# A decoder layer on one core: late stores and sample queries traced later, the sample's mixture split beside the last prompt tiles

## The chip, the cores and the metric

One of the eight cores of a Trainium2 chip runs the whole kernel. The metric is the device time of one execution in microseconds (us). Times before the change: 1391.77 us as the median of three runs (1391.52 to 1400.56).

## What is computed

One step of a decoder layer in float32, for a prompt of 1024 tokens and for a sample group of 8 sequences with 4 new tokens each and 1024 past tokens in paged caches. The model width is 1024.

- The input is normalised (RMSNorm) and multiplied by one combined weight. Its columns are the queries, keys and values of attention A (8 heads of 64), those of attention B (4 heads of 2 x 64, values of 128), and an indexer.
- Attention A is sparse: the indexer's scores select 256 keys for each query, and a softmax runs over these. Attention B is differential: two softmaxes for each head, the second subtracted with a factor lambda, then a norm over each head.
- Both results, the mixture, go through an output weight, and the input is added. That is the residual h.
- h is normalised, and a two-level router picks two of 32 experts for each token. Each expert is a gated feed-forward of width 256. The output is h plus the gated sum.

The new keys and values of both groups are outputs too.

## The kernel before, in words

**Stages.** The first stage (0 to some 470 us) multiplies the input by the combined weight, section by section (BV, I, BK, AV, BQ, AK, AQ), each over eight prompt tiles of 128 tokens and one sample tile of 32. The indexer's selection runs beside the last sections. Then comes the attention stage, then the projection by the output weight and the routing, then the experts.

**Sections.** `evac` takes a section's product for one tile out of PSUM. For queries and keys it computes the norm's factor `rr`, rotates, and multiplies the rotated rows by `rr` (L387): on POOL for the queries of prompt tiles, else on VectorE. `store` puts the result on a list `late` and issues the oldest entries on SP's DMA queue, so that three or four entries lag behind. After the last section (AQ) four entries are left, all of them queries of attention A of tiles 6 and 7, in 256-byte pieces. `open_pages` has already loaded the keys and queries of the first B tile and of the sample (`first`, `sfirst`) and five cache pages (`early`).

**Attention stage.** Two generators run side by side: `prompt_attention("BA")`, eight tiles of B and then eight of A, and `samples()`, the sample's B and then its A attention and after that the output weight. Each yields an estimate of its work, and `mix` always continues the one with the smaller sum, both against the same total.

In `prompt_attention`, `prep` loads a tile's keys (kn, L901) and queries (qn, L903), splits each in a rounded part and a rest and turns them (L404, L920); `probs` forms scores (L936, L937) and exponentials (L940); `turned` transposes these (L876); `values` multiplies by the values (L974 for B, L978 for A). `prep` of the next tile is advanced in steps between a tile's four pairs of heads. After the first tile's `prep` and the first step of the second's, the four late stores are issued (L1041).

In `sample_attention`, the sample's queries and keys are turned (L1080, L1081) and copied into a block matrix QB (L1086) that POOL has zeroed (L1083), and the keys into KN (L1089). Then, for two groups of four sequences: pages of keys are gathered on POOL's queue and turned (L1104), scores are formed (L1112, L1120), the softmax runs over all keys (L1151), its exponentials are transposed by the same L876, and pages of values are multiplied (L1165, and L1169 for the new tokens). At A's end the two groups are reduced (L1179) into `mixS`, B's part lies there already. Then `samples` loads the output weight in sixteen pieces into two buffers (L1219), casts each (L1220) and subtracts the cast from it (L1221), with a yield of 1.5 behind each.

**Projection.** `project` multiplies a tile's mixture by the output weight, both split in two parts (L1325 to L1327). The sample tile is first; the two parts of its mixture (msh, L1282, and msl, L1283) are made at this stage's beginning. Loads of expert weights are spread over this stage on SP's queue.

**What sets the order.** The program is traced once. A planner with a timing model then orders each engine's queue: among the instructions that are ready in its model it takes the one that was traced first. So an instruction that is traced later has a lower rank, but can still be lifted into a gap. `issue_after(x)` keeps what is traced in its block behind x on the same queue. A memory pool that is opened where a closed one lay makes its tiles wait for the last use of what they overlap. Engines work through their queues in that order.

Of the kernel before, what the change touches and what calls it, by code (L numbers as in the profile page):

```python
# [6 lines left out]
F32 = mybir.dt.float32  # L7
# [115 lines left out]
def build(tc, a, upto=99, dbg=None):  # L123
# [248 lines left out]
    def evac(sec, t, ps):  # L372
        r0, n = rows(t)
        att = sec[0]
        if sec[1] in "KQ":
# [7 lines left out]
            if sec[1] == "Q":  # L383

                V.tensor_scalar(rr[:n], rr[:n], 0.125 if t == NT else -0.125, None, op0=ALU.mult)
            E = G if sec[1] == "Q" and t < NT else V
            E.tensor_tensor(out=hd(ko[:n]), in0=hd(ko[:n]), in1=rr[:n].unsqueeze(2).to_broadcast([n, 8, 64]), op=ALU.mult)  # L387
# [495 lines left out]
    def prompt_attention(atts):  # L883
# [153 lines left out]
        yield from advance(1, 1)  # L1037

        while late:
            with tc.issue_after(holds[1]):  # L1040
                Y.dma_start(*late.pop(0))  # L1041
        behind = behind2 = None
        for i in range(len(tiles)):
            cur = nxt
            for u in range(4):
                ex = yield from scores(cur, u)
                if u == 2 and i:
                    last = finish(before)
                    yield next(last)
                if u == 3 and i:  # L1050
                    yield from last
                if behind2:
                    yield from values(*behind2)
                    behind2 = None
                if behind:
                    behind2 = yield from turned(*behind)
                behind = (cur, u, ex)
                yield from advance(i + 1, 2)
# [10 lines left out]
    def sample_attention(att):  # L1069
# [7 lines left out]
        Y.dma_start(vn, vd[att][r0:r0 + NS])  # L1077
        pt = tr()
        for c in range(4):
            T_.transpose(pt[:, c * NS:(c + 1) * NS], qn[:NS, c * P:(c + 1) * P], ident[:NS, :NS])  # L1080
            T_.transpose(pt[:, (4 + c) * NS:(5 + c) * NS], kn[:NS, c * P:(c + 1) * P], ident[:NS, :NS])  # L1081
        QB = sp_.tile([P, 4, 8, 8, 4], F32, name="QB", bufs=1)
        G.memset(QB, 0.0)  # L1083
        for c in range(4):
            for s in range(2):
                V.tensor_copy(QB[64 * s:64 * s + 64, c, :, 2 * c + s, :],  # L1086
                              pt[64 * s:64 * s + 64, c * NS:(c + 1) * NS].rearrange("p (b q) -> p b q", q=4))
        KN = sp_.tile([P, 4, NS], F32, name="KN", bufs=1)
        V.tensor_copy(KN.rearrange("p c n -> p (c n)"), pt[:, 4 * NS:8 * NS])  # L1089
        kc_, vc_ = pages(att, "k"), pages(att, "v")  # L1090
        om = []
        for g in range(2):
            sc = sp_.tile([P, NTOK], F32, name="sc", bufs=1)

            for ch in range(4):
                raws = [early.pop(0) if early else page(kc_, ch, 4 * g + bb) for bb in range(4)]
                kts = []
                for r in range(2):
                    for bb in range(4):
# [6 lines left out]
                        kts.append(kt)  # L1106
                        yield 0.4
                sp = tr()
                for r in range(2):
# [43 lines left out]
            V.tensor_tensor(out=l2[:, 2:3], in0=l2[:, 0:1], in1=l2[:, 1:2], op=ALU.add)  # L1153
            V.reciprocal(l2[:, 3:4], l2[:, 2:3])
            pT = yield from transposed(ex, 8, "pT")
            ptn = tr()
# [45 lines left out]
    p3w = ExitStack()  # L1202
    woh, wol = [], []

    def samples():
# [10 lines left out]
        for k in range(KC):  # L1216
            for q in range(2):
# [4 lines left out]
                yield 1.5  # L1222
        raw.close()

    mix((prompt_attention("BA"), 280), (samples(), 280))
# [53 lines left out]
    sm = p3.enter_context(tc.tile_pool(name="sm", bufs=2, reuse_waits="tile"))  # L1279
    msh = sm.tile([P, 8, NS], F32R, name="msh", bufs=1)  # L1280
    msl = sm.tile([P, 8, NS], F32R, name="msl", bufs=1)
    S.copy(msh, mixS)  # L1282
    V.tensor_tensor(out=msl, in0=mixS, in1=msh.bitcast(F32), op=ALU.subtract)  # L1283
    ovi = cq.tile([P, NT + 1, 2], I32, name="ovi")
# [20 lines left out]
    def project(t):  # L1305
# [9 lines left out]
        else:  # L1315
            mh, ml = msh, msl
        h = fp.tile([P, D], F32, name="xt")
# [309 lines left out]
```

## Time and profile before

| | |
|---|---|
| median of three runs | 1391.77 us |
| the profiled execution | 1403.95 us |
| its span, first to last instruction | 1402.1 us |
| TensorE busy | 1265.0 us, 90% of the span |
| VectorE busy | 792.0 us, 56% |
| ScalarE busy | 561.5 us, 40% |
| POOL busy | 447.8 us, 32% |
| mean granted TensorE clock | 0.960 of full speed |

Busy time is the time in which an engine executes an instruction; register, branch, semaphore and DMA-issuing instructions are not in it. Matmuls are pipelined and their ends are modelled, so a busy TensorE need not be at its peak. The views name TensorE PE, its weight loads PEld, VectorE DVE, ScalarE ACT; SPq is SP's queue. L12 is line 12 of the kernel.

### The profile page before, as it was taken

To read this page: it belongs to the slowest core of one execution; us is meant where nothing else is said; L and a number is where in the kernel's file an instruction comes from. 1 tells how busy PE (TensorE), PEld (TensorE's weight loads), DVE (VectorE), ACT (ScalarE), POOL (GpSimd) and SP (SyncE) were. 2 spreads that over 40 slices of the span, in tenths; PEclk is the share of its full clock that TensorE was granted. 3 is DMA by queue.
4 is the path that set the end of the run, shared out by engine and by line. 5 is a ranking of instruction groups with operands and counts; after the bars stand their busy time and mean duration, and the time that the engine had idled before them with its cause. 6 is when DMAs were issued, how large, how long until landed. Compare 5 with 4: busy or idle time off the path is not lost.

```text
span 1402.1 us, 24778 instructions
## 1 busy us (share of the span) xinstructions
PE 1265.0 (90%) x9359; PEld 855.0 (61%) x9359; DVE 792.0 (56%) x2218; ACT 561.5 (40%) x1239; POOL 447.8 (32%) x505
## 2 busy tenths in 40 slices
PE   7999999997799689898889989999996999999994
PEld 4877675875467576776675776768884333333341
DVE  5544996969987677766655556946754111111110
ACT  5533666895432365544345555732220111111110
POOL 1012233254336534435236544321212112222101
PEclk9999999998899899999899999999997999999997
DMA  6223004133325765666467654347657999999992
GB/s 234 77 88 109 25 24 121 48 109 82 90 97 147 227 244 213 234 210 230 152 227 252 222 161 148 103 135 306 247 172 256 341 370 377 377 381 386 378 340 47
DMA packets 114149, 279.92 MB, mean 200 GB/s; under 512 B 50664, under 2 KB 50920, under 8 KB 101736
## 3 DMA queue, kind: packets, MB, share of 16 engines
q1 hardware_dynamic: 81248, 180.84, 35.4%
q0 software_dynamic: 26272, 95.43, 21.8%
q10 hardware_dynamic: 6504, 2.01, 0.6%
q8 instruction: 75, 1.23, 0.3%
q14 instruction: 50, 0.41, 0.1%
HBM read 234.33 MB, written 43.92 MB: 198 GB/s over the span
## 4 chain that ended last, share of the span: by engine, by line
PE 44%; DMA 9%; DVE 6%; issue 5%; POOL 3%; ACT 2%; SPq 0%; another core or an unknown queue 0%; POOLq 0%; ACTq 0%; DVEq 0%
PE acc L1513 9%; PE S L1533 4%; DMA wg<-in_w_exp_up_dram 4%; PE tr L1104 4%; PE tr L876 3%; PE acc L1325 3%; PE acc L1326 2%; PE acc L1327 2%; PE tr L1112 2%; PE own L1165 2%; PE acc L978 2%; DMA wg<-in_w_exp_gate_dram 2%; PE acc L974 2%; PE tr L936 2%; PE tr L937 2%
## 5 line engine op out<-in xcount | busy, mean ns | idle before, releaser
L532 PE MATMUL acc<-wh,xh 128*128 128x512 f32 x432 | 174.9, 405 | 15.3 <-ACT wh L508 15.3
L1513 PE MATMUL acc<-wg,xT 128*32 128x512 f32 x1536 | 174.7, 598 | 2.8 <-DMA wg<-in_w_exp_up_dram 2.4
L533 PE MATMUL acc<-wh,xl 128*128 128x512 f32 x432 | 172.1, 398 | 0.0
L940 ACT ACTIVATE mk<-mk,mx 128x256 f32<-128x256 f32 (+7 forms) x128 | 99.0, 775 | 83.4 <-DVE mx L938 74.0
L535 PE MATMUL acc<-wl,xh 128*128 128x512 f32 x320 | 126.6, 396 | 0.0
L1513 PEld LDWEIGHTS acc<-wg,xT 128*32 128x32 f32 x1536 | 54.6, 110 | 104.2 <-issue 95.5
L532 PEld LDWEIGHTS acc<-wh,xh 128*128 128x128 f32 x432 | 82.4, 191 | 48.0 <-ACT wh L508 25.8
L1528 DVE COPY aTe<-tr 128x256 f32<-128x256 f32 x24 | 10.2, 425 | 162.6 <-PE tr L1526 162.6
L533 PEld LDWEIGHTS acc<-wh,xl 128*128 128x128 f32 x432 | 82.5, 191 | 17.4 <-issue 1.2
L1533 PE MATMUL S<-wd,aTe 128*32 128x512 f32 x768 | 87.5, 594 | 4.3 <-DVE aTe L1528 3.3
L1508 DVE TENSOR_TENSOR xT<-tr,gc 128x512 f32<-128x512 f32 x48 | 32.9, 688 | 91.5 <-PE tr L1507 91.5
L1104 PE MATMUL tr<-cst,pg 128*128 128x128 f32 x512 | 78.8, 286 | 0.5 <-DVE ql L407 0.4
L936 PE MATMUL tr<-KS,qh 128*128 128x512 f32 (+3 forms) x192 | 75.1, 396 | 1.6 <-DVE aT L864 0.8
L1519 ACT ACTIVATE sg<-acc,its 128x256 f32<-128x256 f32 x24 | 11.4, 474 | 156.0 <-PE acc L1513 156.0
L1537 POOL DMA_INDIRECT out_o_y_dram<-yo,its x24 | 38.0, 1582 | 110.2 <-ACT yo L1536 66.1
L958 POOL TENSOR_SCALAR mk<-mk,rl 128x128 f32<-128x128 f32 (+7 forms) x64 | 49.3, 781 | 70.9 <-DVE rl L950 65.8
L1498 POOL DMA_INDIRECT xg<-s_hn,its x24 | 23.4, 977 | 142.4 <-PE tr L1507 128.9
L876 PE MATMUL tr<-cst,mk 128*128 128x128 f32 x432 | 65.1, 281 | 4.0 <-POOL mk L958 2.4
L535 PEld LDWEIGHTS acc<-wl,xh 128*128 128x128 f32 x320 | 60.9, 190 | 11.8
L937 PE MATMUL tr<-KS,ql 128*128 128x512 f32 (+3 forms) x192 | 66.2, 359 | 0.0
L1536 ACT ACTIVATE yo<-S,its 128x1024 f32<-128x1024 f32 x24 | 26.8, 1115 | 98.5 <-PE S L1533 98.5
L1104 PEld LDWEIGHTS tr<-cst,pg 128*128 128x128 f32 x512 | 61.6, 147 | 6.5 <-issue 2.0
(416 smaller groups left out, 2924.2 us busy)
## 6 DMA issues: line engine op xcount, KB each, us to landing
wg<-in_w_exp_gate_dram SPq DMA_DIRECT2D x32, 1024.0 KB
wg<-in_w_exp_up_dram SPq DMA_DIRECT2D x32, 1024.0 KB
wd<-in_w_exp_down_dram SPq DMA_DIRECT2D x32, 1024.0 KB
wr<-in_w_in_dram SPq DMA_DIRECT2D x56, 256.0 KB
xt<-in_x_prompt_dram SPq DMA_DIRECT2D x16, 512.0 KB
s_mix<-mo SPq DMA_DIRECT2D x16, 256.0 KB
qn<-s_qa SPq DMA_DIRECT2D x8, 512.0 KB
raw<-in_w_out_dram SPq DMA_DIRECT2D x16, 256.0 KB
```

What stands on the lines that cost most here:

```text
L532: T_.matmul(ps, lhsT=xh[t][:, kc, :], rhs=wh[kc], start=kc == 0 and t < NT - 1, stop=False)
L533: T_.matmul(ps, lhsT=xl[t][:, kc, :], rhs=wh[kc], start=False, stop=t == NT - 1 and kc == KC - 1)
L535: T_.matmul(ps, lhsT=xh[t][:, kc, :], rhs=wl[kc], start=False, stop=kc == KC - 1)
L876: T_.transpose(pt[:, (j - b) * P:(j - b + 1) * P], src[:, j * P:(j + 1) * P], ident)
L936: T_.matmul(sp[:, :c1 - c0], lhsT=T.qh[:, h * P:(h + 1) * P], rhs=KS[:, h, c0:c1], start=True, stop=False)
L937: T_.matmul(sp[:, :c1 - c0], lhsT=T.ql[:, h * P:(h + 1) * P], rhs=KS[:, h, c0:c1], start=False, stop=True)
L940: S.activation(mk[:, :W], mk[:, :W], AF.Exp, bias=mx[:, h:h + 1], scale=-1.0, accum_out=T.ll[:, h:h + 1])
L958: G.tensor_scalar(ex[s][:, :W], ex[s][:, :W], T.rl[:, 2 * u + s:2 * u + s + 1], 1.0, op0=ALU.mult, op1=ALU.mult)
L1104: T_.transpose(pt[:, c * P:(c + 1) * P], raws[bb][:, o_:o_ + P], ident)
L1325: T_.matmul(ps[:n], lhsT=mh[:, k, :], rhs=woh[q][k], start=k == 0, stop=False)
L1513: T_.matmul(gu[c:c + m, :].rearrange("p (u f) -> p u f", u=2), lhsT=xT[:, k, c:c + m], rhs=wg[:, :, k, :], start=k == 0, stop=k == KC - 1)
L1533: T_.matmul(py[c:c + m, q * 512:(q + 1) * 512], lhsT=aT[:, k, c:c + m], rhs=wd[:, k, q * 512:(q + 1) * 512], start=k == 0, stop=k == 1)
```

## The change

There are five edits, all of them in order or placement; what is computed stays the same.

- The queries of attention A are multiplied by `rr` on VectorE, where POOL did it.
- The late stores are traced at the beginning of the second prompt tile's scores instead of ahead of the first's, and without `issue_after`.
- The turning of the sample's queries and keys, the zeroing of QB and the copies into QB and KN become a function `queries`, called behind the page transposes of the first chunk of the first group, right ahead of the first score products.
- Between the sample's softmax and the transposes of its exponentials stands a new `yield 7`, so that the prompt's generator is continued there. This happens four times (two attentions, two groups).
- The two parts of the sample's mixture are made at the end of `samples`, in a small pool of their own that is opened on the right side after the pool of the raw weight pieces is closed.

```diff
-            E = G if sec[1] == "Q" and t < NT else V
+            E = G if sec == "BQ" and t < NT else V
...
-        while late:
-            with tc.issue_after(holds[1]):
-                Y.dma_start(*late.pop(0))
         behind = behind2 = None
         for i in range(len(tiles)):
             cur = nxt
+
+            while i == 1 and late:
+                Y.dma_start(*late.pop(0))
...
-        pt = tr()
-        for c in range(4):
-            T_.transpose(pt[:, c * NS:(c + 1) * NS], qn[:NS, c * P:(c + 1) * P], ident[:NS, :NS])
-            T_.transpose(pt[:, (4 + c) * NS:(5 + c) * NS], kn[:NS, c * P:(c + 1) * P], ident[:NS, :NS])
         QB = sp_.tile([P, 4, 8, 8, 4], F32, name="QB", bufs=1)
-        G.memset(QB, 0.0)
...
+        def queries():
+
+            G.memset(QB, 0.0)
+            pt = tr()
+            for c in range(4):
+                T_.transpose(pt[:, c * NS:(c + 1) * NS], qn[:NS, c * P:(c + 1) * P], ident[:NS, :NS])
+                T_.transpose(pt[:, (4 + c) * NS:(5 + c) * NS], kn[:NS, c * P:(c + 1) * P], ident[:NS, :NS])
+            for c in range(4):
+                for s in range(2):
+                    V.tensor_copy(QB[64 * s:64 * s + 64, c, :, 2 * c + s, :],
+                                  pt[64 * s:64 * s + 64, c * NS:(c + 1) * NS].rearrange("p (b q) -> p b q", q=4))
+            V.tensor_copy(KN.rearrange("p c n -> p (c n)"), pt[:, 4 * NS:8 * NS])
...
+                if g == 0 and ch == 0:
+                    queries()
                 sp = tr()
...
+            yield 7
             pT = yield from transposed(ex, 8, "pT")
...
         raw.close()
 
+        mp = p3w.enter_context(tc.tile_pool(name="ms", bufs=1, side="right", reuse_waits="tile"))
+        msh, msl = [mp.tile([P, 8, NS], F32R, name=f"ms{u}") for u in range(2)]
+        S.copy(msh, mixS)
+        V.tensor_tensor(out=msl, in0=mixS, in1=msh.bitcast(F32), op=ALU.subtract)
+        ms.extend((msh, msl))
...
-    msh = sm.tile([P, 8, NS], F32R, name="msh", bufs=1)
-    msl = sm.tile([P, 8, NS], F32R, name="msl", bufs=1)
-    S.copy(msh, mixS)
-    V.tensor_tensor(out=msl, in0=mixS, in1=msh.bitcast(F32), op=ALU.subtract)
```

## Rows read from the trace of the kernel before

**Rows 1.** Busy time by stretch: engines (instructions), granted clock, DMA share, GB/s.
```profile
490.00:931.00 441.00, 396.46 (x3932) 308.71 (x3932) 290.68 (x850) 229.94 (x571) 192.86 (x205) 0.96 0.56 191
931.00:1070.00 139.00, 133.47 (x746) 107.69 (x746) 80.01 (x401) 31.84 (x82) 25.40 (x19) 0.98 0.69 252
...
1079.20:1380.00 300.80, 293.68 (x2524) 110.98 (x2528) 53.82 (x96) 38.31 (x48) 55.43 (x46) 0.99 0.97 354
```

**Rows 2.** TensorE's waits, 463 to 932 us: total us, times, longest.
```profile
PE tr L876 <- ACT sc L1151: 11.6, 4, 5.0
...
PE tr L920 <- ACT le L1034: 7.2, 1, 7.2
PE tr L404 <- DMA qn<-s_qb: 4.9, 1, 4.9
```

**Rows 3.** POOL in order of time: start us, us, instruction, idle before.
```profile
466.91 1.04 POOL L387 TENSOR_TENSOR outl<-outl,rk 128x512 f32<-128x512 f32 x1 [2.45 <-DVE rk L385]
467.91 1.26 POOL L340 TENSOR_TENSOR m<-raw,gtab 128x512 f32<-128x512 f32 x1
...
473.93 1.27 POOL L176 TENSOR_TENSOR kst<-first,kst 128x512 fp32r<-128x512 f32 x1
```

**Rows 4.** Busy time by stretch, behind waits of TensorE; columns as in group 1.
```profile
634.40:637.30 2.90, 2.90 (x14) 2.10 (x18) 1.60 (x5) 0.81 (x3) 0.00 (x0) 0.51 0.00 0
734.40:739.70 5.30, 5.30 (x25) 3.61 (x29) 3.16 (x11) 1.69 (x7) 0.74 (x2) 0.50 0.06 23
832.20:835.20 3.00, 3.00 (x13) 2.81 (x14) 1.08 (x5) 0.83 (x3) 0.00 (x0) 0.50 0.00 0
...
1079.20:1084.40 5.20, 5.14 (x24) 2.36 (x28) 1.39 (x2) 0.00 (x0) 3.20 (x5) 0.50 0.93 321
```

**Rows 5.** TensorE in order of time, around the sample's and the prompt's last products.
```profile
863.90 1.06 PE L1169 MATMUL own<-vns,pn 32*32 32x512 f32 x8
...
866.04 1.65 PE L1179 MATMUL tr<-cst,om 128*128 128x32 f32 x14
...
900.36 0.39 PE L937 MATMUL tr<-KS,ql 128*128 128x512 f32 x1
...
928.89 1.96 PE L978 MATMUL acc<-aT,VV 128*64 128x128 f32 x30
931.83 0.42 PE L1325 MATMUL acc<-woh,msh 128*32 128x512 f32 x1 [0.98 <-ACT msh L1282]
```

**Rows 6.** Line 387: ns min/median/max, first and last start us, shapes.
```profile
L387 DVE TENSOR_TENSOR outl<-outl,rk x12: 670/692/1776, 144.1 to 435.0; 128x512 f32<-128x512 f32 x8, 32x512 f32<-32x512 f32 x4
...
L387 POOL TENSOR_TENSOR outl<-outl,rk x8: 1044/1046/1418, 324.7 to 472.0; 128x512 f32<-128x512 f32 x8
```

**Rows 7.** Busy time in section AQ; columns as in group 1.
```profile
425.00:468.00 43.00, 42.92 (x200) 34.68 (x200) 30.54 (x82) 12.11 (x27) 27.90 (x28) 1.00 0.56 142
```

**Rows 8.** SP's queue in order of time: issue us, us, instruction.
```profile
467.98 0.51 SPq L1041 DMA_DIRECT2D s_qa<-outl  x1
...
473.38 0.71 SPq L903 DMA_DIRECT2D qn<-s_qb  x1
```

**Rows 9.** The chain of waits, in order of time: start us, us, what.
```profile
473.38 11.65 DMA qn<-s_qb
```

**Rows 10.** Line 1086; columns as in group 6.
```profile
L1086 DVE COPY QB<-tr x16: 172/194/1264, 474.0 to 679.2; 64x32 f32<-64x32 f32 x16
```

**Rows 11.** Line 1221; columns as in group 6.
```profile
L1221 DVE TENSOR_TENSOR wol<-raw,woh x16: 670/736/1279, 870.5 to 905.9; 128x512 fp32r<-128x512 f32 x16
```

**Rows 12.** VectorE in order of time, the last subtraction but one.
```profile
903.59 1.09 DVE L1221 TENSOR_TENSOR wol<-raw,woh 128x512 fp32r<-128x512 f32 x1 [0.30 <-ACT woh L1220]
```

**Rows 13.** ScalarE in order of time: one cast, and the mixture's first part.
```profile
874.45 0.62 ACT L1220 CAST woh<-raw 128x512 fp32r<-128x512 f32 x1
...
931.37 0.41 ACT L1282 CAST msh<-mixS 128x256 fp32r<-128x256 f32 x1
```

**Rows 14.** SP's queue, the issue of a piece of the output weight.
```profile
871.64 0.33 SPq L1219 DMA_DIRECT2D raw<-in_w_out_dram  x1
```

More of the change, by code (lines that the diff above doesn't have):

```diff
@@ L1077, in sample_attention @@
         Y.dma_start(vn, vd[att][r0:r0 + NS])
-        pt = tr()
-        for c in range(4):
-            T_.transpose(pt[:, c * NS:(c + 1) * NS], qn[:NS, c * P:(c + 1) * P], ident[:NS, :NS])
-            T_.transpose(pt[:, (4 + c) * NS:(5 + c) * NS], kn[:NS, c * P:(c + 1) * P], ident[:NS, :NS])
         QB = sp_.tile([P, 4, 8, 8, 4], F32, name="QB", bufs=1)
-        G.memset(QB, 0.0)
[L1084 to L1087, printed above, removed]
-        KN = sp_.tile([P, 4, NS], F32, name="KN", bufs=1)
-        V.tensor_copy(KN.rearrange("p c n -> p (c n)"), pt[:, 4 * NS:8 * NS])
+        KN = sp_.tile([P, 4, NS], F32, name="KN", bufs=1)
+        def queries():
[9 more added lines that the diff above has]
+            V.tensor_copy(KN.rearrange("p c n -> p (c n)"), pt[:, 4 * NS:8 * NS])
         kc_, vc_ = pages(att, "k"), pages(att, "v")
@@ L1202, in build @@
     p3w = ExitStack()
-    woh, wol = [], []
+    woh, wol, ms = [], [], []
     def samples():
@@ L1315, in project @@
         else:
-            mh, ml = msh, msl
+            mh, ml = ms
         h = fp.tile([P, D], F32, name="xt")
```

## The prediction

> **What bounds the kernel now.** I read the busy time by stage first [rows 1]. In the attention stage (490 to 931 us) TensorE is busy 396.5 of 441 us, in the projection after it 133.5 of 139, in the experts' stage 293.7 of 300.8. Every engine before the projection feeds TensorE, and the two stages behind it have next to no idle time in it: whatever moves the first matmul of the projection (931.83) moves the end by as much, as long as the loads of expert weights, which are queued behind the same stage, move along. So I look only for idle time of TensorE ahead of 931.83, and for new idle time there.
>
> Second, the waits of TensorE from 463 to 932 [rows 2]. Three of them are what the change aims at. The transposes of the sample's exponentials (L876 on sc) wait four times for the exponential on ScalarE, 11.6 us together, once 5.0. At the start of the stage TensorE waits 7.2 us ahead of the first key transposes (L920), which the view puts down to ScalarE but whose input kst is made on POOL at 473.93 [rows 3], and 4.9 us for the load of the second tile's queries (qn).
>
> Third, the granted clock behind such waits [rows 4]: 0.51, 0.50, 0.50 of full speed in the 2.9, 5.3 and 3.0 us that follow three of the four waits, with TensorE busy all the time, that is 1.2 instead of 2.4 GHz. A wait thus costs its length and half of the slow stretch: (2.9 + 5.3 + 3.0) / 2 = 5.6 us.
>
> **Part 1: yield 7 ahead of the transposes.** Tracing order is settled by the two generators' yields, and I summed these. The prompt's sum to 209.1 units. The sample's summed to 180.8 (156.8 of attention and 24 for the output weight) and now sum to 208.8, since four times 7 is added. Behind the sample's last product, 52.3 units of the prompt fill the 66 us from 865 to 931 [rows 5], 1.26 us each, so seven units are some 9 us of prompt work. In front of one such wait TensorE had nothing else for at most 5.0 us, so the seven units cover it. What can be gained is 11.6 + 5.6 = 17.2 us; the least I allow is 10.6, one us of waiting left and no gain in clock. I take 15, near the upper end, since the gap filled is longer than the longest wait. What is late next in those places is the transposes' evacuation ahead of the L1165 products, as now.
>
> **Part 2: AQ's scaling from POOL to VectorE.** Eight POOL instructions of 1.046 us become eight on VectorE of 0.69 us [rows 6]. VectorE is busy 30.5 of 43 us in this section and TensorE 42.9 of 43 [rows 7], so 5.5 us more on VectorE lie under matmuls. Only the end shows: the sixth tile's scaling ran on POOL at 466.91 and the next rotation waited behind it until 467.91 [rows 3]; now that rotation, and kst behind it, can start some 2 us sooner. That shortens the 7.2 us wait, but TensorE then stands longer for qn, which is issued at 473.38 [rows 8] and takes 11.65 us to land [rows 9]. So the price of this part is what qn's landing moves by. The store at the head of SP's queue waits for that POOL instruction and goes at 467.98 [rows 8]; with VectorE's 0.69 it would go 0.4 us sooner.
>
> A rule speaks against this part. One DVE scaling took 1.776 us where the median is 0.692 [rows 6]: something held it for 1.1 us, at least once in twelve. The Trainium skill (SBUF — State Buffer, Who interferes with whom) says that a VectorE instruction with two SBUF inputs and a GpSimd instruction that reads SBUF exclude each other for a whole instruction; by that the last scaling could stand behind a 1.26 us rotation and the sum below would be some 0.9 us worse. The median in the row says that this is rare here.
>
> **Part 3: the late stores.** They are four stores of the A queries of the last two such tiles (L1041), issued on SP from 467.98 on [rows 8], around the loads of VV, vns, kn and qn. Traced at the second tile they stand behind VV, kn and qn of the second tile in rank. But the planner hands SP whatever is ready in its model, and the first store was ready before the loads, or it would not stand at the head. I expect the first two to stay there and the last two to go at about the same place. Nothing reads them until the A tiles, some 250 us later. Parts 2 and 3 together: at best the wait of 4.9 us goes, at worst one more POOL instruction's time, 1.0 us, is lost, as a store of tile 7 slips ahead of qn. I take 1 us gained, near the end at which qn's place in the queue stays.
>
> **Part 4: the queries behind the first chunk's transposes.** The same eight small transposes, eight copies of 0.194 us [rows 10] and a larger one to KN now stand right ahead of the score products (L1112) that read them, twice, once per attention. If nothing else is ready TensorE waits 8 x 0.194 = 1.55 us and, for KN and the handovers, half as much again (an estimate from the same row), 2.3 us each time, 4.6 in all; if the planner lifts them into a gap, nothing. The memset of QB leaves POOL's queue ahead of kst, but that again ends in the wait for qn. The query page of attention B is held longer, which delays one page gather by as much; the pages wait behind it on POOL's queue. I take 1 us lost: the copies need only a loaded tile and a free bank, so they can be lifted, but perhaps not both times.
>
> **Part 5: where the sample now ends.** This is the term that decides. In the kernel before, the sample's last product (L1169, ends 864.96) lies in the sixth A tile, its output weight is converted by 906.6 [rows 11], and the prompt's last product ends at 930.85 [rows 5]: 24 us of slack. By the yields, L1169 now comes right behind the first two scores of the last tile, whose products ended at 900.75 [rows 5]. From there TensorE has 930.85 - 900.75 = 30.1 us of prompt work, and the sample's reduction (L1179, sixteen products in some 2.1 us, fourteen of them in 1.65) [rows 5].
>
> Behind L1169 hangs a chain that TensorE does not set. Sixteen pieces of the output weight are loaded into two buffers, cast on ScalarE and subtracted on VectorE. From the first subtraction (870.5) to the last (905.9) a piece took 35.4 / 15 = 2.36 us [rows 11]. The last but one ends at 904.68 [rows 12], 39.7 us behind L1169. The two parts of the sample's mixture are traced behind the sixteenth piece, and their pool is opened on the side and in the place that the raw buffers held; so the first part (0.41 us on ScalarE [rows 13]) cannot be written before the raw buffer is free. Now the numbers. With parts 1 to 4 the prompt's last product ends at 930.85 - 15 - 1 + 1 = 915.85. L1169 ends 32.2 us ahead of that, at 883.65. The first part is there at 883.65 + 39.7 + 0.41 = 923.8, and the projection, whose first matmuls take the sample's mixture, starts there: 8.0 us of idle TensorE where 0.98 is now [rows 5], and 8.0 us sooner than 931.83. Behind an idle time of this length the clock stood at 0.50 for 5.2 us [rows 4], which takes 2.6 back. At the fastest the pieces could follow at 2.05 us: a load issued at 871.64 [rows 14] was cast from 874.45 on [rows 13], so 2.8 us, with 0.62 and 0.67 of work a buffer is free again after 4.1, and there are two. That takes 14 x 0.31 = 4.3 off the chain, and the idle time is 3.6. At the slowest the mixture waits for the sixteenth piece, 1.9 us later, and the idle time is 9.9.
>
> **The sum**: -15 (waits and clock) -1 (stage start) +1 (queries) +7.0 (8.0 less the 0.98 of now) +2.6 (clock) = -5.4 us. The profiled execution took 1403.95 us (span 1402.1), the median of the runs shown is 1391.77, 12.2 less; I take the difference in us over to the median: **1386.4**. With all bounds at their best, -17.2 - 4.9 + 0 + 2.6 + 1.5 = -18.0 (1374); at their worst, -10.6 + 1.0 + 4.6 + 8.9 + 2.7 = +6.6 (1398), where 1.5 and 2.7 are half of the shortest and longest slow stretch [rows 4].
>
> **Rivals.** (a) The chain of part 5 costs nothing: the planner lifts the sample's work, or the mixture's two parts get memory of their own and are made early, and the projection's first matmuls need only the early pieces. Then -15, 1376.8, and with a shorter wait for qn 1373. For it: the conversions waited little, and the first matmuls take pieces in order. Against it: 2.36 us a piece and 32 us of TensorE work. 0.25.
>
> (b) Slower: the sample's end slides into the prompt's end. Its last products wait for page gathers on POOL, and if these come behind the last tiles' scalings in that queue, the planner lets prompt products pass and L1169 slips; each us of slip is a us of idle TensorE, as the chain of 39.7 us follows it. It decides from 19 us of slip on (1% slower); with L1169 at the very end of the prompt it is 32 us, 1418. For it: both generators now end within 0.3 units of each other, so no slack is left. Against it: such gathers hold TensorE nowhere among the longer waits [rows 2]. 0.13.
>
> (c) The change does not do what it says: the planner, which picks by readiness, leaves the transposes where they were, and the waits stay. Then only parts 2 and 3, 1390.8. It would need prompt work not to be ready in its model. 0.07. My forecast keeps 0.55.
>
> **How the numbers follow.** A measurement of this kernel can tell about 1% (13.9 us) from no change. Forecast and (c) lie within it, 0.62 with their edges; (a) lies mostly below 1377.9, and with the forecast's own lower edge makes 0.25; (b) 0.13. The range goes from (a) with the shorter wait, 1373, to the forecast's worst, 1400.
>
> **What would show it.** Right: the waits of L876 on sc gone from the view of waits; full clock behind them; the last conversion (L1220, L1221) ending behind the prompt's last product (L978); the first L1325 waiting 3 to 10 us for the mixture, with the clock at 0.50 behind it. Wrong: L1325 right behind L978 (a); L1169 within a few us of the last L978 (b); L876 still waiting for the exponentials (c). Part 3 is wrong if qn is issued ahead of the first late store, part 4 if L1112 waits over 2 us for QB.

## The result, and the profile after

The changed kernel takes 1401.80 us (median of ten runs, 1397.68 to 1410.47), the kernel before, on the same chip, 1395.08 (ten runs, 1391.52 to 1400.56). The ratio is 1.0052, 95% interval 1.0034 to 1.0070: 6.7 us slower, where 5.4 us less were forecast, and 1.8 us above the range's upper end. It lies within the 1% that was named as the limit of what can be told at the prediction; ten runs a side tell it, and so does another chip, where the ratio is 1.0048 (1.0030 to 1.0066); on a third, G below, it is 1.0012.

One caution first. The profiled execution of before took 1403.95 us, more than any of its ten runs; that of after took 1402.70, near its median. The two traces of the first chip thus differ by -1.25 us where the medians differ by +6.7. Below, the two are used for single waits; sums are taken from pairs of runs on other chips.

The stages after, columns as in group 1 of before [rows 1]:

```profile
490.00:931.00 441.00, 394.17 (x3868) 307.77 (x3865) 289.44 (x842) 227.56 (x565) 192.69 (x204) 0.96 0.57 192
931.00:1070.00 139.00, 133.89 (x742) 107.27 (x739) 77.97 (x399) 31.16 (x80) 25.36 (x19) 0.97 0.65 237
1079.20:1380.00 300.80, 294.03 (x2532) 109.02 (x2534) 53.70 (x96) 36.98 (x47) 56.34 (x46) 0.99 0.97 354
```

TensorE is about as busy in the attention stage as before. The waits, from 463 to 940 us, show why: total us, times, longest.

```profile
PE acc L1334 <- ACT ms L1234: 7.8, 1, 7.8
PE tr L1117 <- issue: 7.6, 19, 1.0
PE tr L1001 <- DVE bo L997: 6.0, 3, 3.0
PE tr L1206 <- DVE bo L1203: 5.4, 1, 5.4
PE tr L920 <- POOL kst L176: 3.7, 1, 3.7
...
PE tr L876 <- DVE mk L955: 3.1, 2, 2.0
PE tr L876 <- POOL mk L958: 2.9, 2, 2.0
PE tr L404 <- DMA qn<-s_qb: 2.8, 1, 2.8
...
PE tr L1117 <- DVE QB L1089: 1.9, 2, 1.1
```

Against [rows 2]: the four waits for the exponentials (sc) are gone, the two at the stage's start are down from 7.2 and 4.9 us to 3.7 and 2.8. In their place stand the norm at the end of a B tile (bo, L997), a longer wait for the same norm at the end of the sample's B (L1203), and 7.8 us ahead of the first weight product (L1334, the old L1325). The sample's norm had 3.2 us in the kernel before:

```profile
PE tr L1199 <- DVE bo L1196: 3.2, 1, 3.2
```

TensorE at the end of the attention stage, in order of time, and ScalarE's first part of the mixture:

```profile
880.77 1.06 PE L1176 MATMUL own<-vns,pn 32*32 32x512 f32 x8
...
918.00 2.86 PE L978 MATMUL acc<-aT,VV 128*64 128x128 f32 x32
928.68 0.63 PE L1334 MATMUL acc<-woh,ms 128*32 128x512 f32 x1 [7.82 <-ACT ms L1234]
```

```profile
926.85 0.62 ACT L1227 CAST woh<-raw 128x512 fp32r<-128x512 f32 x1 [2.59 <-DMA raw<-in_w_out_dram]
...
928.23 0.40 ACT L1234 CAST ms<-mixS 128x256 fp32r<-128x256 f32 x1 [0.76 <-DVE wol L1228]
```

The sample's last product (L1176, the old L1169 [rows 5]) ends at 881.83, and the mixture's first part waits for the sixteenth piece of the weight. The five us behind the wait, columns as in group 1, run at 0.50 of the clock:

```profile
928.70:933.70 5.00, 5.00 (x12) 2.00 (x13) 0.39 (x1) 0.00 (x0) 0.00 (x0) 0.50 1.02 359
```

At the stage's start the load of qn is issued 3.9 us sooner than in [rows 8]. SP's queue, issue time first:

```profile
464.58 0.51 SPq L1043 DMA_DIRECT2D s_qa<-outl  x1
...
469.45 1.13 SPq L903 DMA_DIRECT2D qn<-s_qb  x1
471.73 1.44 SPq L1043 DMA_DIRECT2D s_qa<-outl  x2
```

### The profile page after: what moved, and what is told of

It reads as the page before. It is cut to its first block, busy times and chain, and to the rows that moved or that the text cites. A ratio compares the mean times of both kernels' runs of the same rounds, so it can differ in the third digit from the quotient of the medians.

```text
span 1400.9 us, 24782 instructions
## 1 busy us (share of the span) xinstructions
PE 1267.1 (90%) x9359; PEld 855.5 (61%) x9359; DVE 794.8 (57%) x2226; ACT 560.3 (40%) x1239; POOL 441.0 (31%) x497
## 3 DMA queue, kind: packets, MB, share of 16 engines
q1 hardware_dynamic: 81248, 180.84, 35.6%
## 4 chain that ended last, share of the span: by engine, by line
PE 48%; DMA 10%; DVE 6%; issue 4%; ACT 2%; POOL 1%; SPq 0%; POOLq 0%; DVEq 0%; ACTq 0%
PE acc L1522 9%; PE S L1542 4%; DMA wg<-in_w_exp_up_dram 4%; PE tr L1107 4%; PE tr L876 3%; PE tr L1117 3%; PE acc L1334 3%; PE acc L1335 2%; PE acc L1336 2%; PE acc L978 2%; DMA wg<-in_w_exp_gate_dram 2%; PE acc L974 2%; PE own L1172 2%; PE tr L936 2%; PE tr L937 2%
## 5 line engine op out<-in xcount | busy, mean ns | idle before, releaser
L864 DVE COPY aT<-tr 128x512 f32<-128x512 f32 (+3 forms) x86 | 46.1, 555 | 48.8 <-PE tr L876 35.3
L958 POOL TENSOR_SCALAR mk<-mk,rl 128x128 f32<-128x128 f32 (+7 forms) x64 | 49.2, 779 | 65.6 <-DVE rl L950 37.4
L535 PEld LDWEIGHTS acc<-wl,xh 128*128 128x128 f32 x320 | 60.8, 190 | 11.8
```

Source lines behind the costliest of these rows:

```text
L535: T_.matmul(ps, lhsT=xh[t][:, kc, :], rhs=wl[kc], start=False, stop=kc == KC - 1)
L864: V.tensor_copy(out, in_)
L958: G.tensor_scalar(ex[s][:, :W], ex[s][:, :W], T.rl[:, 2 * u + s:2 * u + s + 1], 1.0, op0=ALU.mult, op1=ALU.mult)
```

## The experiments

Each run was compared with runs of the kernel before on its own chip, where that one took 1372.9 to 1374.6 us, but for four runs marked G, on a chip where it took 1401.45. All ratios:

| run | what it is | ratio (95%) |
|---|---|---|
| r0_before | before, unedited | 0.9996 (0.9983 to 1.0009) |
| r2_after | changed kernel | 1.0048 (1.0030 to 1.0066) |
| e1_no_yield | changed, no yield | 0.9980 (0.9967 to 0.9992) |
| r2_no_yield | the same, on r2_after's chip | 0.9992 (0.9981 to 1.0002) |
| e4_yield_only | before + yield 7 | 1.0051 (1.0038 to 1.0065) |
| e2_parts_late | changed, parts of the mixture made late | 1.0034 (1.0021 to 1.0047) |
| e3_yield_half | changed, yield 3.5 | 1.0024 (1.0012 to 1.0036) |
| e9_yield_rescaled | changed, sample's total 323 | 0.9968 (0.9957 to 0.9980) |
| e5_scaling_only | before + scaling on VectorE | 0.9957 (0.9944 to 0.9971) |
| r2_scaling, r3_scaling | the same, two chips | 0.9969, 0.9969 (0.9957 to 0.9981) |
| e7_queries_only | before + queries later | 1.0030 (1.0018 to 1.0042) |
| r3_no_queries_rescaled | e9 without the queries | 0.9968 (0.9956 to 0.9980) |
| e12_scores_halved | e5 + score batches of 32 | 1.0096 (1.0082 to 1.0111) |
| G: r1_after | changed kernel | 1.0012 (1.0000 to 1.0024) |
| G: e6_stores_only | before + late stores | 0.9977 (0.9962 to 0.9993) |
| G: e10_no_queries_rescaled | e9 without the queries | 0.9993 (0.9974 to 1.0012) |
| G: e11_scaling_yield_rescaled | before + scaling, yield, 323 | 1.0000 (0.9981 to 1.0018) |

**Is it the yield?** The first run is the kernel before; the others are the changed kernel, the same without the yield, and the kernel before with the yield alone.

> The kernel before itself, to see how far one profiled execution stands from the timed runs. Theory A (the record's sum, made against one profiled execution, carries over to the median): its profile lies within 2 us of the first one, 1403.95. Theory B (that first profile was a slow execution): its profile lies near the timed median, 1392 to 1398, and the time missing lies in one stretch that can be named by comparing the two traces (stage start, experts' stage). The ratio to itself is 1.000 within 0.002.

```diff
-            yield 7      (e1_no_yield, r2_no_yield: from the changed kernel)
+            yield 7      (e4_yield_only: into the kernel before)
```

> The changed kernel without the yield of 7, all else kept. Theory A (the chain of weight conversions behind the sample's last product costs what the changed profile shows, 7.8 us of idle TensorE and 2.5 us of half clock, and the yield is what puts it there): the sample ends in the sixth A tile again, the wait for ms ahead of the first weight product falls below 1.5 us, the four waits for the exponentials come back (9 to 12 us), and the earlier start of the stage stays: 1387 to 1394, ratio to before 0.993 to 0.999. Theory B (the loss comes from the edits at the stage's start): 1398 or more.

> The changed kernel once more, as the base for the next run on the same chip. If no batch of score products waits for issue here, the parts should add up: 1.002 to 1.0045. If they wait for issue (7 to 12 us): 1.0005 to 1.006, the span of the two chips so far.

> The changed kernel without the yield of 7. If the yield costs the same on every chip, this is 0.0045 to 0.007 below r2_after in ratio. Rival (where the score products wait for issue, the yield's pause costs less, as prompt work then fills the longer way to the exponentials): 0 to 0.004 below r2_after.

> The kernel before with nothing but the yield of 7 ahead of the transposes of the sample's exponentials. Theory A (the pause itself costs: it opens new waits of TensorE on the prompt's own chains, and more stretches at 0.50 of the clock, as the run with 3.5 units showed with only 36.7 us idle but 58 us at half clock): slower, ratio 1.003 to 1.008, with waits of L1001 or L974 on DVE bo L997 of 4 us or more. Theory B (only the late end of the sample and the output weight's chain cost): the parts of the mixture are made at the projection's start here, so the chain binds as well: 1.002 to 1.006, with 5 to 9 us of waiting on msh ahead of the first weight product, and no other loss. Rival C (the yield gains alone and loses only together with the other four edits): 0.990 to 0.998.

It is. r0_before could not decide between its theories, since it ran on a chip where the kernel takes 20 us less. r2_after, 1.0048, came out just above what the added parts gave (1.0045 at most). Without the yield the changed kernel stands at 0.9980 on one chip and at 0.9992, within its interval of no change, on another; with it, on the second chip, it is 8.5 us slower (1380.17 against 1371.72). Alone on the kernel before it costs 0.51%, 7.0 us by the ratio. Theory A and theory B both allow that number; the trace of e4_yield_only has 6.4 us of waiting on msh, as B says, but also 6.7 us on bo (L1001), so B's "no other loss" fell. Waits of TensorE in r2_no_yield:

```profile
PE tr L876 <- ACT sc L1156: 11.9, 4, 4.5
...
PE tr L1205 <- DVE bo L1202: 3.2, 1, 3.2
...
PE tr L876 <- POOL mk L958: 2.4, 5, 0.7
...
PE tr L876 <- DVE mk L955: 1.3, 2, 1.1
...
PE tr L1001 <- DVE bo L997: 0.7, 1, 0.7
```

and in r2_after:

```profile
PE acc L1334 <- ACT ms L1234: 7.6, 1, 7.6
PE tr L1001 <- DVE bo L997: 6.7, 4, 3.0
PE tr L1206 <- DVE bo L1203: 6.6, 1, 6.6
...
PE tr L876 <- DVE mk L955: 3.6, 4, 2.0
PE tr L876 <- POOL mk L958: 3.5, 3, 2.0
```

The yield takes 11.9 us of waits away and brings 7.6 for the mixture's parts, 6.0 (6.7 less 0.7) for the norms of prompt tiles, 3.4 for the sample's norm and 3.4 for the masks: 20.4. The same two runs from 468 us to the first weight product, columns as in group 1:

```profile
468.00:899.83 431.83, 395.78 (x3982) 315.22 (x3982) 306.08 (x884) 238.41 (x587) 202.18 (x214) 0.96 0.61 209
```

```profile
468.00:906.17 438.17, 393.15 (x3982) 315.80 (x3982) 302.13 (x883) 235.32 (x587) 202.20 (x213) 0.95 0.61 208
```

Idle time rises from 36.0 to 45.0 us, and the stretch by 6.3. (The first stage's last product ended at 464.78 and 463.68; counted from there it is 10.1 and 7.4 us.) The spans differ by 10.3 (1369.9, 1380.2), so some 4 more are lost behind that product. There the clock stays at 0.50 for 5.6 us, which accounts for 2.8. Half clock sums to 37.6 us in r2_no_yield and to 51.2 in r2_after. Both have a long slow stretch at the stage's start; the longest others of r2_after begin in the wait for the sample's norm, in the second of two waits of 1.8 and 2.0 us, and in the wait for the parts:

```profile
672.80:683.00 10.20, 7.37 (x32) 6.12 (x33) 4.80 (x12) 1.42 (x8) 2.05 (x2) 0.50 0.01 2
887.90:894.70 6.80, 5.48 (x38) 4.82 (x39) 1.74 (x4) 2.83 (x7) 2.65 (x2) 0.50 0.39 119
901.50:911.70 10.20, 5.53 (x13) 2.21 (x14) 1.96 (x6) 1.52 (x3) 0.00 (x0) 0.50 0.98 321
```

**Is it only the late end?** e2 makes the parts where the kernel before made them, e3 halves the yield.

```diff
 # e2_parts_late: in samples(), the pool of ms is not opened; at the projection's start
     V.tensor_tensor(out=msl, in0=mixS, in1=msh.bitcast(F32), op=ALU.subtract)
+    ms.extend((msh, msl))
 # e3_yield_half
-            yield 7
+            yield 3.5
```

> The changed kernel with the two parts of the sample's mixture made at the projection's beginning again, the yield of 7 kept. Theory A (TensorE waits because the two parts stand behind the sixteenth weight piece): the parts are made as soon as the prompt ends, the first weight products use early pieces, the idle time ahead of them falls from 7.8 to under 2 us, 1391 to 1395, ratio 0.996 to 1.000. Theory B (the chain itself binds, wherever the parts are made, since the projection needs its last pieces): the wait moves to a later weight product, the time gained is under 3 us, ratio 1.002 to 1.006.

> The changed kernel with a yield of 3.5 in place of 7, one number. Theory A (the chain needs 43 us of the prompt behind the sample's last product): 14 units or some 17 us are given back to the end, so 32 + 17 = 49 us are left and the chain fits; no wait for ms over 1.5 us; the waits for the exponentials stay below 5 us together; 1388 to 1393, ratio 0.994 to 0.999. Theory B (any yield there costs, since it only moves waits): 1398 or more.

In e2 the first weight product still waits 7.0 us for msh: where the parts are made makes no difference that shows, since the last cast of a piece (904.13) stands ahead of msh (904.65) on ScalarE there too. In e3 the end is free: the first weight product starts at 909.05, and the prompt's last products run until 909.12. Yet it is still slower than e1. Its waits:

```profile
PE acc L974 <- DVE bo L997: 5.6, 3, 4.1
...
PE tr L876 <- DVE mk L955: 3.3, 3, 2.0
...
PE tr L876 <- ACT sc L1156: 2.7, 2, 1.5
```

Here is less idle time than in r0_before (36.7 against 40.1 us, from 468 us to the first weight product), but the stretches at half clock sum to 58 us where r0_before has 34. Against e1, which differs in the yield alone, it has 1.1 us more idle time (36.7, 35.6) and 21 us more of half clock (58, 37). So the theory that the late end alone costs fell.

**The yield without its lateness.** Seven units at four places make the sample's sum 28 units longer, and the weighing of the two generators then lets all its work lie later beside the prompt. Raising its total by the same share takes that back.

```diff
-    mix((prompt_attention("BA"), 280), (samples(), 280))
+    mix((prompt_attention("BA"), 280), (samples(), 323))
```

> The changed kernel with its yield of 7, but the sample's generator is weighed against a total of 323 in place of 280, so that its 208.8 units end as early beside the prompt as the 180.8 did: the last L1169 product should lie in the sixth or seventh A tile, 20 us or more ahead of the prompt's last product than in the changed kernel, and the output weight's chain is free. Theory A (the pause itself costs, by new waits and stretches at half clock): no faster than the kernel before, 1.000 to 1.005. Theory B (only the late end costs): the gain of the removed waits shows at last, 0.987 to 0.996.

> The changed kernel without the queries traced later and with the sample's total at 323, on another chip. If the parts add (queries +0.30% off the run with the total of 323 alone, 0.9968): 0.992 to 0.9955, and below r3_scaling. Rival (the pause gives nothing beyond the scaling, wherever the sample ends): within 0.0015 of r3_scaling, or above it.

> The kernel before with the scaling alone, as measured twice: 0.9945 to 0.998.

e9 missed both of its theories: it is faster than before, but by less than theory B named. In its trace the sample's last product ends at 829.36, 64 us ahead of the prompt's last (893.19), about where it ends with the scaling alone (830.07 in r3_scaling). It is 0.8% below the changed kernel (on another chip): the loss was the lateness, and by e3 not only at the prompt's end. (The new weighing without the yield was not run.) But the removed waits gave nothing that shows. On one chip r3_no_queries_rescaled stands at 0.9968 and r3_scaling, which has neither yield nor new weighing, at 0.9969, so the rival holds; on e9's own chip the scaling alone (e5) has 0.9957. That e9, with the queries traced later, stands at 0.9968 as well means that their 0.30%, measured alone below, does not simply add. Waits of r3_no_queries_rescaled, and the two stretches from 468 us to the first weight product (r3_scaling first):

```profile
PE tr L876 <- POOL mk L958: 5.4, 3, 4.2
PE tr L920 <- POOL kst L176: 4.2, 1, 4.2
PE tr L876 <- DVE mk L955: 4.0, 5, 1.4
```

```profile
468.00:897.11 429.11, 392.32 (x3974) 312.09 (x3974) 306.55 (x884) 237.39 (x588) 201.21 (x213) 0.96 0.61 210
```

```profile
468.00:896.27 428.27, 396.99 (x3981) 316.68 (x3979) 308.15 (x887) 238.47 (x588) 202.02 (x214) 0.96 0.62 211
```

Idle time falls from 36.8 to 31.3 us, with the masks of an A tile (L958, on POOL) as the new long wait, but the products take 4.7 us more, of which the clock explains nothing (34 us of half clock in both). Counted from the end of the first stage's last product (464.10, 465.82) it is 6.5 us less idle time, 3.9 more in the products, and a stretch 2.6 shorter. The pair e5 and e9, where that product ended at the same time (462.95, 462.91), has 5.1 less, 4.7 more, and 0.4 shorter. Why the products take longer is open. By the time from one product's start to the next, waits left out, L978 has 1.8 of the 3.9 us and no other line over 1.2, and no run takes them apart.

**The other parts alone.**

```diff
-            E = G if sec[1] == "Q" and t < NT else V
+            E = G if sec == "BQ" and t < NT else V
```

> The kernel before with nothing but the scaling of attention A's queries on VectorE. Theory A (the gain of 1.9 us without the yield comes from here, since the store at the head of the queue of SP waits for the last scaling, and qn behind it): qn is issued 3 to 4 us sooner, ratio 0.996 to 0.999. Rival (the gain comes from the stores or the queries traced later): qn is issued within 1 us of the run of the kernel before, 0.9995 to 1.0015.

> The kernel before with the scaling alone. If the 4.7 us by which qn lands sooner reach the end on every chip: 0.994 to 0.998. Rival (the time is given back to the score products' issue where these wait): 0.998 to 1.001.

Three chips give 0.9957, 0.9969 and 0.9969: 4.3 to 5.9 us, the only part whose gain shows on more than one chip. VectorE's queue before (first fence, trace of the kernel before) and in r2_scaling shows why it is so much:

```profile
464.49 0.69 DVE L342 TENSOR_TENSOR raw<-raw,gtab 128x512 f32<-128x512 f32 x1 [1.82 <-POOL m L340]
...
466.66 0.17 DVE L385 TENSOR_SCALAR rk<-rk 128x8 f32<-128x8 f32 x1
...
469.21 0.69 DVE L342 TENSOR_TENSOR raw<-raw,gtab 128x512 f32<-128x512 f32 x1 [1.79 <-POOL m L340]
```

```profile
463.50 0.17 DVE L385 TENSOR_SCALAR rk<-rk 128x8 f32<-128x8 f32 x1
463.70 0.69 DVE L387 TENSOR_TENSOR outl<-outl,rk 128x512 f32<-128x512 f32 x1
```

VectorE waited 1.8 us a tile for POOL's half of the rotation (m, L340), which stood on POOL behind the scaling of the tile before, and that waited for VectorE's rk. Taking the scaling off POOL opens this ring: TensorE's wait ahead of L920 begins at 468.04 and 467.63 in the two traces, and rk of the sixth tile is made 3.2 us sooner, 2.8 when counted from these two points. The first late store follows it, and qn behind that:

```profile
464.43 0.51 SPq L1041 DMA_DIRECT2D s_qa<-outl  x1
...
469.21 0.62 SPq L903 DMA_DIRECT2D qn<-s_qb  x1
```

e7 traces the queries later, with the function `queries` of the change and nothing else; e6 only the late stores.

> The kernel before with nothing but the turning of the sample's queries traced behind the first chunk's page transposes. As predicted for this part: 0 to 4.6 us lost, ratio 1.000 to 1.0035, with waits of the score products on QB of 1 to 4 us. Rival (the small transposes traced later free the first tile's start, and this is what gained 1.9 us without the yield): 0.996 to 0.999.

> The kernel before with nothing but the late stores traced at the second tile. By the prediction, which left these stores at their place in the queue of SP, and by the difference of the parts (-0.07%): 0.998 to 1.001, qn issued within 1 us of the kernel before. Rival (the stores are what frees qn's place): qn 2 us sooner or more, 0.996 to 0.998.

e7 loses 0.30%, 4.1 us. In r0_before the eight small transposes ran at 462.3 us under the last section's products. In e7 they come at 487.6, right ahead of the score products, with the wait for QB, and a stretch at half clock follows:

```profile
489.56 0.65 PE L1118 MATMUL tr<-kts,QB 128*32 128x128 f32 x8 [0.83 <-DVE QB L1090]
...
490.55 2.66 PE L1118 MATMUL tr<-kts,QB 128*32 128x128 f32 x56
```

```profile
489.10:492.50 3.40, 2.94 (x49) 2.30 (x53) 1.80 (x9) 0.00 (x0) 0.43 (x1) 0.50 1.02 394
```

The wait on QB, 0.83 us, stays below the 1 us that was the least expected. The loss lies within the price forecast, but half clock has more part in it (3.4 us, a cost of 1.7) than the wait; the rest, 1.6 us, is not accounted for. e6 gained 3.2 us on chip G (0.9977), just past the 0.998 at which the expectation ended, so its ratio is the rival's. The rival's mechanism is not there: qn is issued 8.8 us behind the start of the first stage's last product (472.83, 464.00), and 8.7 behind it in the kernel before (473.38, 464.70). It lands 10.1 us after its issue where it took 11.8, and TensorE's wait for it is 3.4 us where [rows 2] have 4.9. No trace of the unchanged kernel is from that chip, so what gained the 3.2 us is open.

**Chip G.** Here, as on the first chip (it may be the same one), the kernel before takes some 20 to 28 us more than on the four others; in the two traces of before, nearly all of the difference lies in the attention stage.

> The changed kernel itself, unedited, beside the others on one chip. If the parts add up as measured one by one (yield +0.51%, scaling -0.43%, queries +0.30%, the rest by difference -0.07%): ratio 1.002 to 1.0045. If the parts work on each other: above 1.005 (the first chip gave 1.0052) or below 1.001.

> The changed kernel without the queries traced later, and with the sample's total at 323. If the queries' 0.3% is the half clock and the wait on QB at the stage's start and adds to the rest: 0.992 to 0.9955, the fastest so far. Rival (the earlier start only moves the same waits on, as the queries' loss did not show in the run with the rescaled total): 0.996 to 0.998, as that run.

> The kernel before with the scaling on VectorE, the yield of 7 and the sample's total at 323: neither stores, queries nor the mixture's parts are moved. If the scaling (-0.43%) and the placed yield (-0.12%, the run with 323 against the run without yield) add: 0.993 to 0.996. Rival (with the wait for qn gone the yield has nothing left to give, or costs): 0.996 to 0.999, no faster than the scaling alone.

> The scaling alone, and each batch of 64 score products traced as two of 32, each behind its own four page transposes, with a copy of 128 columns behind each half. Theory (a batch of 64 narrow products, four of them side by side on TensorE, is more than the instruction supply can follow): where batches wait for issue, these waits fall from some 11 us to under 5, and the ratio is 0.002 to 0.006 below r2_scaling. Rival (the gaps hang on something else than the length of a batch): issue waits within 2 us of r2_scaling, ratio within 0.002 of it or above. Where no batch waits for issue, both say within 0.003 of r2_scaling.

```diff
 # e12_scores_halved, on e5: r = 0 and r = 1 each with their own transposes, products and copy
-                    T_.matmul(sp[32 * bb:32 * bb + 32, r * P:(r + 1) * P], ...
+                        T_.matmul(sp[32 * bb:32 * bb + 32, :P], ...
```

The changed kernel stands at 1.0012 here, between its two expectations (1.002 and up if the parts add, below 1.001 if they work on each other). Its interval does not meet the first chip's (1.0034 to 1.0070), so even if the two are the same chip the loss is not the same. e10 and e11, which were to gain, stand at 0.9993 and 1.0000: their expectations missed, the rivals' too. TensorE gets the batches of 64 narrow score products with gaps on the first chip and on G. The idle time before L1112, in the trace of before on the first chip (us, times):

```profile
  issue: 10.8, 20
  DVE kts L864: 0.6, 2
```

and in r0_before, on another, no row with "issue":

```profile
  DVE kts L864: 0.8, 2
```

In e11 the row is 13.7 us in 30 times, in r1_after 7.7 in 21. That may be why the parts are worth something else here, but it is argued, not shown: e12 was to test it and ran on a chip that has no such gaps. There it lost 1.3% against the scaling alone, where 0.3% at most was expected, because 1024 score products in batches of 32 keep TensorE busy for 50.5 us instead of 35.3 (e5). So what the gaps hang on is open, and so is the scaling's worth on such a chip, where it was not run alone.

## Why the prediction was wrong

- **Part 1, -15 us: this step failed.** The mechanism it names happened: the waits on sc are gone in every kernel with the yield of 7, and rival (c) with it. What failed is the sentence on what is late next, "the transposes' evacuation ahead of the L1165 products, as now". I asked which wait the prompt's work would fill, and not which waits the sample's work had filled until then. With the sample paused, a B tile's norm (ScalarE, POOL, VectorE, then L1001), the sample's norm and the masks stand bare: 12.8 us of new waits (6.0, 3.4, 3.4) for the 11.9 removed. With the lateness taken back, the idle time falls by 5.5 us, and the products take 4.7 more. Either way next to nothing is left of the 15. The 5.6 us of clock did not come back either: on r2_after's chip half clock rose by 13.6 us with the yield, at the new waits, and with the lateness taken back it stayed at 34 us.
- **Parts 2 and 3, -1 us: mis-sized.** With the scaling alone the two waits fell from 7.2 to 4.2 and from 4.9 to 0.9 us (r2_scaling), 7.0 together, and 4.3 to 5.9 reach the end: about the better bound of 4.9 or past it. The step that failed is "with VectorE's 0.69 it would go 0.4 us sooner": it exchanged two durations, 1.05 for 0.69, and left the scaling's start where it was. Counted from the start of the first stage's last product, that store went 3.1 us sooner in r2_scaling, and qn 3.8. The idle 2.45 us ahead of it [rows 3] belonged to a ring of POOL and VectorE that the change opens. The order on SP's queue came as forecast. One thing weighed against it came and cost nothing that shows: in the trace after, one of the eight scalings took 1.83 us, from 454.74 on, while POOL ran a rotation from 454.73 to 456.02; the last tile's took 0.72. In r2_scaling one took 1.80, in r3_scaling none more than 0.98, and both stand at 0.9969. By the Trainium skill (SBUF — State Buffer, Who interferes with whom) a VectorE instruction with two SBUF inputs and a GpSimd (POOL) instruction that reads SBUF exclude each other. The 1.83 agrees: the scaling ended 0.55 us after the rotation, which is most of its usual 0.69.
- **Part 4, +1 us: mis-sized.** 4.1 us in e7, within the bounds of 0 and 4.6, but by luck: the bound was made of two waits of 2.3 us for the copies, and the trace has one of 0.83, half clock, which the term did not hold, and 1.6 us that are not accounted for. The planner did not lift the transposes into the gap ahead of qn. As a term it was 3 us off.
- **Part 5, +9.6 us: the mechanism right, the size by luck.** Forecast: the sample's last product ends at 883.65, the projection starts 8.0 us late at 923.8, with 5.2 us of half clock. In the trace: 881.83, 7.82 us, 928.68, 5.0 us. But two errors cancel. The prompt's work behind the sample's last product took 39.0 us (until 920.86), not 32.2: 5.4 us of waits instead of the 2.0 behind 900.75 in the kernel before, and 6.8 us at half clock. The chain took 46.8 us (until 928.63), not 40.1, and longer than its slow bound of 42.0: it needed the sixteenth piece, its first subtraction began 6.4 us behind the sample's last product instead of 5.5, and the pieces followed at 2.62 us instead of 2.36. ScalarE's casts waited longer for the pieces to land, before and after (us, times):

```profile
  DMA raw<-in_w_out_dram: 1.9, 4
```

```profile
  DMA raw<-in_w_out_dram: 10.7, 8
```

  On r2_after's chip the term is 6.6 us of idle time and some 4 behind it, 10.6 in all.
- **The sum.** On r2_after's chip parts 1 and 5 together are the yield's 8.5 us. Then 8.5 - 4.3 to -5.9 + 4.1 gives +6.7 to +8.3, against +6.7 on the first chip and +6.6 on r2_after's. How the 8.5 divide is known less well: the 10.6 of part 5 come from two traces that lie 10.3 us apart, which leaves -2 to 0 for part 1. The parts also do not quite add (the queries' 4.1 us are missing in e9), and the stores were measured on chip G only.
- **Rivals.** (a) fell: the first weight product waits. (b) fell: the sample's last product ends 39 us ahead of the prompt's last. The price of (c), 1390.8, had left out part 4's 1 us. The slower side was reached by the forecast's own part 5 with part 1 gone, a combination that the rivals did not hold: its price stood in the sum as +9.6, and part 1's lower bound, 10.6, was set as if only the size of the gain were unknown.
- **The base.** Carrying the sum's difference over in us assumed that the profiled execution was like the others. It was 9 us above the median of ten, so the profile pair shows next to nothing of the loss. The base of three runs, 1391.77, was itself 3.3 us below the median of ten. On that median the loss of 6.7 us is what the sum has with all bounds at their worst, +6.6: that the time lies past the range's end is the base, that it lies on the slower side is part 1.

The version that gains most for the least is the scaling alone: 0.31 to 0.43% under the kernel before on three chips. Nothing added to it gained more there.

## What to carry to other kernels

When a pause fills one generator's wait with another's work, list what the paused work was covering, and price those waits as well: here 11.9 us of waits went, 12.8 came, and only a balance restored elsewhere kept the pause free of loss. A yield also moves everything behind it, so check where the last piece of work ends and what chain hangs on it. When an instruction moves to another engine, follow the ring of waits through both queues rather than exchange two durations.

## What the runs showed of the hardware

- The same program takes 1373 to 1375 us on four chips and 1395 to 1401 on the first and on G; in the two traces of before, the score products that are handed over with gaps of up to 1 us ("issue", 10.8 us in 20 times against none) also keep TensorE busy longer (42.6 us against 35.3).
- The sum of TensorE's waits does not tell what they cost: e3 has 3.4 us less idle time than r0_before, and 24 us more at half clock. Traces of one program differ less: the scaling alone has 27, 34 and 34 us of half clock on three chips.
- A short step of VectorE lasted over several instructions of POOL. The last 128x8 scaling of rk (L385) usually takes 0.17 us; in the three traces of the scaling alone it took 2.83 to 2.85, while POOL ran a gather, the memset of QB and a product for kst one after the other, and it ended within 0.1 us of the last of them. No run tests what held it.
